# Latent tiles in the tables' loop and six normalisation tiles in the recurrence's last chunks

## The chip, the core and the metric

The kernel runs on one core of a Trainium2 chip. The metric is the device time of one execution in microseconds; of several runs the median counts. Engines are named as in the profile: PE is TensorE, PEld its weight loads, DVE is VectorE, ACT is ScalarE, POOL is GpSimd, SP is SyncE, which only starts DMAs here.

## What is computed

Two layers of a first block, then one layer of a second block (which the change doesn't touch), over 1024 tokens of width 1024; the first block works on T = 1040 tokens, 16 of them learned. A layer of the first block projects each token to 1920 + 448 features, feeds 448 of them to latent attention (four heads) and the rest to a recurrence that runs over the tokens in both directions (eight heads of 64 x 64 state), joins the two, and goes through a mixture of experts. The parts that matter here:

```python
proj = h @ w_in[li]
c_q, c_kv, k_pe, rw = _split(proj, [Q_LORA, KV_LORA, QK_ROPE, RWKV_COLS])   # 256, 128, 64, 1920
y_att = _mla(c_q, c_kv, k_pe, ...)          # rms norms of c_q and c_kv, rope of k_pe, softmax attention
u = p + mu_prev * (prev - p) + mu_next * (nxt - p)       # p = rw, shifted by a token both ways
r, k, v, wd_f, wd_b, ad_f, ad_b, gd = _split(u, [...])   # 512 each for r, k, v; 64 each; 128
v = v + (v_first - v) * sigmoid(v0 + (v @ v1) @ v2)      # in the second layer only
g = sigmoid(gd) @ g2
kk = k * k_k; kk = kk * rsqrt(sum(kk * kk, heads) + 1e-12)
for each direction:
    decay = exp(-exp(-softplus(-(w0 + tanh(wd) @ w2)) - 0.5)); a = sigmoid(a0 + ad @ a2)
    kd = k * (1 + (a - 1) * k_a)
    S = S * w_t - (S kk_t) (kk_t a_t)' + v_t k_t';  y_t = S r_t          # over the tokens
    bonus = sum(r * kd * r_k) * v
y = y_f + y_b; yn = (y - mean) * rsqrt(var + eps) * gn_g + gn_b          # by head
out = (yn + bonus_f + bonus_b) * g
```

## The kernel before

Features lie on partitions, tokens along the free axis. `proj` works in *feature tiles* of 128 columns of `w_in`. `ftile` splits a weight tile into a high and a low part (`pw_hi` on ACT, `pw_lo` on DVE) and makes 72 matmuls of 128 x 348 (three token thirds, eight steps of the inner dimension, three products of high and low parts), in one of the two PSUM buffers of tag `mm`. `shifted` copies the sum to SBUF on ACT (`pt`) and makes the shift by a token of three DVE steps: times `c0`, plus `mup` times the left neighbour, plus `mun` times the right one (L388 to L393). `plain` is `ftile` with a copy alone.

The order in `proj`: tiles 12 and 13 (`wd`, `ad`); then `dirs` with the k tiles 4 to 7, the norms of kk (`unit_keys`: `kk_ps`, a reciprocal, and `kkb_ps` with 12 products that scale all four kk), and the *tables' loop* over f = 0 to 3. A pass of it has the r tile f and, for both directions d, the low-rank products `low_ps` (first of `wd`, giving `lg`, then of `ad`, giving `ta`), a scan over the tokens (`cum`), an exponential (`P`), and the tables AR and BK, made by DVE and POOL, which ACT's queue stores to DRAM. The last DVE steps of a pass add and multiply kd (L612, L613), and PE's `bo` takes the bonus sum from them. After the loop come the v tiles 8 to 11 and `values`: in layer 1 the residual chain of v (a DMA of `vf`, two small products, a sigmoid and three DVE steps for each of the four tiles), then transposes `v_ps` of v forwards and reversed (`vr`, by POOL), copied by ACT and stored by ACT's queue. `latent` stands last: the tile of the rotary key (`kr`), tile 14 (the gate), the compressed keys' tile (`ck`) and two of compressed queries (`cq`), and between them, at the end of a tile's third third, the gate's rows `g_ps`, the norm of ck (`ck_ps`, a reciprocal) and the rotary product (`kp_ps`). This whole part is ordered by a scheduler that looks at priorities in program order and at free buffers.

`recur` is ordered by hand for PE, ACT, DVE and SP (`manual_schedule`); POOL is not in that list. It runs over N = 17 chunks of 64 tokens, one chunk of each direction at a time. Within a chunk c stand the state's product (`Rp`), the solve (`Wp`), own and next products (`dS`, and on DVE the state S, L968), and the output `Yp`, copied as `ys` by ACT and stored as `d_y` by POOL's queue. Beside them `r_inv` inverts the triangular blocks of four later chunks at once, in 31 double steps on DVE (L876, L877) and three transposes (Z, TF, TT). `turn` hands out these steps by an estimated time:

```python
left = turn(inv, left, 2.2)      # after C["solve"]
left = turn(inv, left, 0.8)      # after C["next"]
left = turn(inv, left, 99.0 if c % GRP == GRP - 1 else 5.2)   # after C["out"]; GRP = 4
```

`r_prep` builds blocks six and more chunks ahead, so the last chunks have none. `r_load` clears half of `uv` on POOL and loads the rest on SP's queue. After the loop `r_post` is called for nine token tiles (tile 0 has 16 tokens, the others 128): it loads both directions' y (POOL's queue), v and g (SP's), adds, takes mean and variance by head (DVE reduces, POOL subtracts, ACT squares and takes a root), scales, adds the bonus and multiplies by g, on DVE and POOL in turn, and stores `yr`. The scheduler places these steps among those of `mla`, the attention that follows, whose heads each run over nine query tiles (`ms` scores on PE, `mx` on DVE, Exp on ACT, `ptp` transposes).

## Time and profile before

| what | us |
| --- | --- |
| median of three runs | 4390.46 (4386.04 to 4396.25) |
| the profiled execution | 4402.54 |
| its span in the trace | 4400.7 |
| PE busy in it | 3830.7 (87%) |
| DVE busy | 2767.7 (63%) |
| ACT busy | 1869.7 (42%) |
| POOL busy | 988.2 (22%) |

The page gives each engine's busy time, a picture of the span in 40 slices, the DMA queues, the chain of work that ended last and the costliest groups of instructions. For a change that touches four stages the busy shares of the whole span say little; what counts is which engine is full in each stage, and which wait ends last. In layer 0 the k tiles and the loop lie between about 80 and 282 us, the projection's tail up to 402, the recurrence up to 679, the attention's heads from 725 on; in layer 1 the loop ends at 1819, the tail at 1969. A row of the timeline merges neighbours of one kind (x6 is six of them); the bracket behind it is the idle time of the engine before it and what ended that. An fp32 product stands in the trace as two matmuls.

### The profile page before, as it was taken

The numbers are of one execution on the slowest core, as the hardware profiler recorded it, in microseconds if no ns is written. First come the engines' busy times: TensorE is split into PE (matmuls) and PEld (weight loads), VectorE is DVE, ScalarE is ACT, GpSimd is POOL, SyncE is SP. The second block draws the span as 40 slices with busy tenths as digits, with TensorE's granted clock in tenths as the row PEclk, the third lists the DMA queues.
The fourth block names the chain that finished last, engine by engine and source line by source line (L and its number), as shares of the span: only waits on it lengthen the run. The fifth ranks groups of instructions, "written<-read, shape, count | busy, mean of one in ns | idle before, by whom it ended". The sixth has DMA issues, their size and how long they took to land. (4 is left out here: it accounts for less than half of the span.)

```text
span 4400.7 us, 68329 instructions
## 1 busy us (share of the span) xinstructions
PE 3830.7 (87%) x27155; PEld 3157.1 (72%) x27155; DVE 2767.7 (63%) x4684; ACT 1869.7 (42%) x3033; POOL 988.2 (22%) x719
## 2 busy tenths in 40 slices
PE   7888897899699688897887896997898889999998
PEld 7677676786576476776776775765786677888786
DVE  7763777757698757627668577997644753333354
ACT  4323445542387543233555532876424522111232
POOL 2331124201242243311233012331422410000000
PEclk9788798999799887886988997999998899999999
DMA  4446663113499833447641043998521121111232
GB/s 154 101 129 183 160 161 108 37 54 128 160 345 346 300 102 101 115 143 172 165 125 58 1 172 131 340 335 309 181 73 29 53 97 58 48 48 43 90 126 81
DMA packets 384153, 611.94 MB, mean 139 GB/s; under 512 B 50467, under 2 KB 217602, under 8 KB 381762
## 3 DMA queue, kind: packets, MB, share of 16 engines
q1 hardware_dynamic: 278402, 485.38, 35.3%
q10 hardware_dynamic: 85200, 70.97, 5.4%
q0 software_dynamic: 20224, 51.15, 3.7%
q8 instruction: 216, 3.54, 0.3%
q14 instruction: 111, 0.91, 0.1%
HBM read 491.65 MB, written 123.45 MB: 140 GB/s over the span
## 5 line engine op out<-in xcount | busy, mean ns | idle before, releaser
L252 DVE TENSOR_TENSOR w13l<-xw,w13h 128x1024 fp32r<-128x1024 f32 x248 | 296.4, 1220 | 57.5 <-ACT w13h L251 53.9
L251 ACT ACTIVATE w13h<-xw 128x1024 fp32r<-128x1024 f32 x256 | 267.4, 1058 | 130.3 <-PE x_hp L258 76.6
L256 PE MATMUL pp_ps<-T_hi,pw_hi 128*128 128x348 f32 x912 | 309.7, 340 | 8.7 <-ACT T_hi L1752 2.9
L257 PE MATMUL pp_ps<-T_lo,pw_hi 128*128 128x348 f32 x912 | 305.4, 335 | 1.4 <-DVE T_lo L1757 1.3
L258 PE MATMUL pp_ps<-T_hi,pw_lo 128*128 128x348 f32 x912 | 304.3, 334 | 0.0
L2414 PE MATMUL f_mm<-F_hi,f_wh 128*128 128x512 f32 x704 | 222.8, 398 | 1.7 <-ACT F_hi L251 1.7
L2414 PE MATMUL f_mm<-F_lo,f_wh 128*128 128x512 f32 x704 | 222.6, 397 | 0.0
L2414 PE MATMUL f_mm<-F_hi,f_wl 128*128 128x512 f32 x704 | 222.3, 397 | 0.0
L256 PE MATMUL x_hp<-w13h,x_h 128*96 128x512 f32 x512 | 208.5, 407 | 0.1
L257 PE MATMUL x_hp<-w13l,x_h 128*96 128x512 f32 x512 | 204.7, 400 | 0.0
L258 PE MATMUL x_hp<-w13h,x_l 128*96 128x512 f32 x512 | 204.0, 398 | 0.0
L256 PEld LDWEIGHTS pp_ps<-T_hi,pw_hi 128*128 128x128 f32 x912 | 179.8, 197 | 21.8 <-issue 7.8
L257 PEld LDWEIGHTS pp_ps<-T_lo,pw_hi 128*128 128x128 f32 x912 | 179.8, 197 | 5.1 <-DVE T_lo L1757 2.6
L287 POOL TENSOR_TENSOR g_x<-g_x,g2g 128x1024 f32<-128x1024 f32 x6 | 14.3, 2385 | 750.4 <-ACT g_x L284 750.4
L258 PEld LDWEIGHTS pp_ps<-T_hi,pw_lo 128*128 128x128 f32 x912 | 179.5, 197 | 3.0 <-issue 3.0
L252 DVE TENSOR_TENSOR f_wl<-F_raw,f_wh 128x1024 fp32r<-128x1024 f32 x44 | 53.7, 1221 | 203.2 <-ACT f_wh L251 203.2
L251 ACT ACTIVATE f_wh<-F_raw 128x1024 fp32r<-128x1024 f32 x44 | 46.4, 1060 | 307.0 <-PE f_mm L2414 301.4
L1616 POOL DMA_INDIRECT d_y<-x_o,r_idx x64 | 102.8, 1606 | 312.1 <-DVE x_al L252 288.8
L825 PE MATMUL aa<-ar_p,bk_p 64*128 64x128 f32 x1088 | 134.0, 376 | 40.2 <-DVE A L827 33.6
L2414 PEld LDWEIGHTS f_mm<-F_hi,f_wh 128*128 128x128 f32 x704 | 133.1, 189 | 34.4 <-ACT F_hi L251 2.0
L2414 PEld LDWEIGHTS f_mm<-F_lo,f_wh 128*128 128x128 f32 x704 | 132.7, 189 | 32.8 <-DVE F_lo L252 0.6
L2414 PEld LDWEIGHTS f_mm<-F_hi,f_wl 128*128 128x128 f32 x704 | 132.9, 189 | 32.4
(630 smaller groups left out, 11221.3 us busy)
## 6 DMA issues: line engine op xcount, KB each, us to landing
xw<-in_moe_w SPq DMA_DIRECT2D x256, 512.0 KB
xw<-in_moe_w SPq DMA_DIRECT2D x64, 1024.0 KB
wd_raw<-in_w_down SPq DMA_DIRECT2D x44, 512.0 KB
pw_raw<-in_w_in SPq DMA_DIRECT2D x36, 512.0 KB
d_AR<-AR ACTq DMA_DIRECT2D x32, 544.0 KB
d_BK<-BK ACTq DMA_DIRECT2D x32, 544.0 KB
ar_p<-d_AR SPq DMA_DIRECT2D x68, 256.0 KB
bk_p<-d_BK SPq DMA_DIRECT2D x68, 256.0 KB
```

The costliest lines, as they stand in the source:

```text
L251: nc.scalar.activation(hi, src, AF.Copy)
L252: (lo_eng or nc.vector).tensor_tensor(lo, src, hi.bitcast(F32), ALU.subtract)
L256: mm(out, wh, xh, start=first, stop=False)
L257: mm(out, wh, xl, start=False, stop=False)
L258: mm(out, wl, xh, start=False, stop=last)
L287: e1.tensor_tensor(out[:n], out[:n], gb[:n], ALU.mult)
L825: nc.tensor.matmul(aa[d][:, h - z], bk[q, h], ar[q, h], start=True, stop=True)
L1616: nc.gpsimd.indirect_dma_start(out=y2[:, :], out_offset=bass.IndirectOffsetOnAxis(ap=si, axis=0), in_=y, in_offset=None, bounds_check=2 * ...
L2414: nc.tensor.matmul(p[:, j], a[:, k], b[:, k, 512 * j:512 * j + 512], start=st, stop=sp)
```

## The change

- `shifted`: the product with `c0` moves from DVE to a second ACT copy that reads PSUM, with a scale.
- Four latent tiles (two of `cq`, `ck`, `kr`) move from the end of the projection into the loop: `compressed` is a generator, and each pass of the loop takes one tile from it after its first direction. `ck` and `kr` go to DRAM (`raw`) and are read back by `latent`. Each cq tile sums its squares by itself (`sqs`).
- The loop's beginning: the low-rank products run ahead, `lg` one direction ahead (two buffers), `ta` as soon as its buffer is free. The norms of kk stand ahead of the first r tile, and a pass scales its own kk alone.
- `latent` stands ahead of the v tiles, with loads and POOL's rope; the norm of ck and the rotary product run within v tile 1. Tile 14 follows the v tiles, the gate's rows stand between the forward transposes. The transposes are copied by DVE with four buffers and stored by SP's queue.
- `r_post` is a generator of four stages. Six tiles (4, 5, 3, 6, 2, 7) begin in chunks 10 to 15; every chunk takes a stage of each tile under way after `C["out"]` and another after the inverse's last turn. The add of both directions moves from POOL to DVE, the store of `yr` from ACT's queue to POOL's. Tiles 1, 8 and 0 follow the loop.

```diff
-                nc.vector.tensor_scalar(u, pt[:, 1:T + 1], p["c0"][:, j:j + 1], None, ALU.mult)
+                nc.scalar.activation(u.rearrange("p (q n) -> p q n", q=3), ps, AF.Copy, scale=p["c0"][:, j:j + 1])
+                u = u[:, :T]
...
+                self.dirs(li, p, S, psp, up, kp, shifted, wd, ad, lw, self.compressed(p, S, psp, up, cp, ftile))
             with self.tpool(name="p_v", bufs=1) as vp:
-                vt = [shifted(8 + f, vp.tile([128, T], F32, name=f"vt{f}", tag=f"val{f}")) for f in range(4)]
-                self.values(li, vt, p, S, psp, up, vp)
-                self.latent(li, p, S, psp, up, vp, shifted, ftile)
-
-    def latent(self, li, p, S, psp, up, vp, shifted, ftile):
+                norm, rotated, gate = self.latent(li, p, S, psp, up, vp, shifted)
+                vt = [shifted(8 + f, vp.tile([128, TP], F32, name=f"vt{f}"), {0: norm, 1: rotated} if f == 1 else {}) for f in range(4)]
+                gated = gate()
+                self.values(li, vt, p, S, psp, up, vp, gated)
...
+    def compressed(self, p, S, psp, up, cp, ftile):
...
+        for f in range(2):
+            a = plain([(128 * f, 128, 0)])
+            x = up.tile([128, TP], F32, name="u")[:, :T]
+            nc.scalar.activation(x, a, AF.Square)
+            sqs = psp.tile([128, 9, 2], F32, name="sqs", tag="tp")
+            for i, (c, n) in enumerate(TT):
+                nc.tensor.matmul(sqs[:n, i], x[:, c:c + n], self.ones32[:, 0:2], start=True, stop=True)
+            nc.scalar.activation(cqs[:NM, f, 0:1], sqs[:NM, 0, 0:1], AF.Copy)
+            nc.scalar.activation(cqs[:, f, 1:9], sqs[:, 1:9, 0], AF.Copy)
+            nc.vector.tensor_scalar(a, a, p["qn"][:, f:f + 1], None, ALU.mult)
+            nc.scalar.dma_start(S["cq"][f], a)
+            yield
+        for i, cols in enumerate(([(256, 128, 0)], [(384, 64, 0), (416, 32, 64), (384, 32, 96)])):
+            nc.scalar.dma_start(S["raw"][i], plain(cols))
+            yield
...
+        def decay(f, d):
+
+            lg = low(wd, lw["w2"], f, d, "lg", p[f"w0{d}h"], 2)
+            nc.gpsimd.tensor_scalar(lg, lg, -0.5 * CDEC, -0.5 * CDEC, ALU.mult, ALU.add)
+            return lg
+
+        def rate(f, d):
+            return low(ad, lw["a2"], f, d, "ta", p[f"a0{d}h"], 1)
...
+        ahead, ta1 = decay(0, 0), rate(0, 0)
+        norms()
         for f in range(4):
-            r = shifted(f, up.tile([128, T], F32, name="u"), {} if f else {0: norms, 2: scaled})
-            k, kk = kt[f], kkt[f][0]
+            k, kk = kt[f], scaled(f)
+            r = shifted(f, up.tile([128, TP], F32, name="u"))
             kds = []
             for d in range(2):
+                lg, ta = ahead, ta1
+                if f + d < 4:
+                    ahead = decay(f + d, 1 - d)
...
+                    ta1 = rate(f + d, 1 - d)
...
+                if d == 0:
+                    next(between)
...
-        def scaled():
-            for f in range(4):
-                for c, n in NC3:
-                    rb = psp.tile([128, 512], F32, name="kkb_ps", tag="tp")
-                    nc.tensor.matmul(rb[:, :n], self.pairpick[:, 128 * f:128 * f + 128], rn[:, c:c + n], start=True, stop=True)
-                    nc.vector.tensor_tensor(kt[f][0][:, c:c + n], kt[f][0][:, c:c + n], rb[:, :n], ALU.mult)
+        def scaled(f):
+            kk = kp.tile([128, T], F32, name="kk", bufs=2)
+            for c, n in NC3:
+                rb = psp.tile([128, 512], F32, name="kkb_ps", tag="tp")
+                nc.tensor.matmul(rb[:, :n], self.pairpick[:, 128 * f:128 * f + 128], rn[:, c:c + n], start=True, stop=True)
+                nc.vector.scalar_tensor_tensor(kk[:, c:c + n], kt[f][:, c:c + n], p["kk"][:, f:f + 1], rb[:, :n], ALU.mult, ALU.mult)
+            return kk
...
+                vs = vp.tile([128, RW], F32, name="v_sb", bufs=4)
+                nc.vector.tensor_copy(vs[:n], vp_ps[:n])
+                nc.sync.dma_start(S["v"][rev][c:c + n, :], vs[:n])
+                if not rev:
+                    next(gated)
...
+                order, rows = [4, 5, 3, 6, 2, 7, 1, 8, 0], []
+                rest = [self.r_post(R, i) for i in order]
+
+                def norms(c, new=False):
+                    if new and 10 <= c < 16:
+                        rows.append(rest.pop(0))
+                    for r in list(rows):
+                        if next(r, 0) == 0:
+                            rows.remove(r)
...
                     C["out"]()
+                    norms(c, True)
                     next(late, None)
                     if P:
                         P["diag"]()
                     left = turn(inv, left, 99.0 if c % GRP == GRP - 1 else 5.2)
+                    norms(c)
...
-        nc.gpsimd.tensor_tensor(y0[:n], y0[:n], y1[:n], ALU.add)
         yv = y0[:n].rearrange("p (h v) -> p h v", h=8)
         y1v = y1[:n].rearrange("p (h v) -> p h v", h=8)
         vv = v[:n].rearrange("p (h v) -> p h v", h=8)
         mu = tp.tile([128, 8], F32, name="q_mu")
+        vr = tp.tile([128, 8], F32, name="q_vr")
+        nc.gpsimd.tensor_tensor(vv, vv, S["bonus"][:n, i, :, None].to_broadcast([n, 8, 64]), ALU.mult)
+        nc.gpsimd.tensor_tensor(v[:n], v[:n], bb[:n], ALU.add)
+        yield
+        nc.vector.tensor_tensor(y0[:n], y0[:n], y1[:n], ALU.add)
         nc.vector.tensor_reduce(mu[:n], yv, AX.X, ALU.add)
         nc.vector.tensor_scalar(mu[:n], mu[:n], 1.0 / 64, None, ALU.mult)
         nc.gpsimd.tensor_tensor(yv, yv, mu[:n, :, None].to_broadcast([n, 8, 64]), ALU.subtract)
+        yield
         nc.scalar.activation(y1[:n], y0[:n], AF.Square)
-        vr = tp.tile([128, 8], F32, name="q_vr")
         nc.vector.tensor_reduce(vr[:n], y1v, AX.X, ALU.add)
+        yield
         nc.scalar.activation(vr[:n], vr[:n], AF.Sqrt, scale=1.0 / 64, bias=self.eps["gn"][:n])
         nc.vector.reciprocal(vr[:n], vr[:n])
-        nc.gpsimd.tensor_tensor(vv, vv, S["bonus"][:n, i, :, None].to_broadcast([n, 8, 64]), ALU.mult)
-        nc.gpsimd.tensor_tensor(v[:n], v[:n], bb[:n], ALU.add)
         nc.vector.tensor_tensor(yv, yv, vr[:n, :, None].to_broadcast([n, 8, 64]), ALU.mult)
         nc.vector.tensor_tensor(y0[:n], y0[:n], gb[:n], ALU.mult)
         nc.vector.tensor_tensor(y0[:n], y0[:n], v[:n], ALU.add)
         nc.gpsimd.tensor_tensor(y0[:n], y0[:n], g[:n], ALU.mult)
-        nc.scalar.dma_start(S["yr"][c0:c0 + n, :], y0[:n])
+        nc.gpsimd.dma_start(S["yr"][c0:c0 + n, :], y0[:n])
```

How the change stands in the program, at the places that the prediction speaks of. TensorE, layer 0, between the r tiles of pass 1 and pass 2 before (`pp_ps` are matmuls of feature tiles, `low_ps` low-rank products; the second s_wd row belongs to the other direction):

```order
L258 MATMUL pp_ps<-T_hi,pw_lo 128x348
L563 MATMUL low_ps<-s_wd,r_w_652 128x348 x3
L563 MATMUL low_ps<-s_ad,r_a_654 128x348 x3
L563 MATMUL low_ps<-s_wd,r_w_652 128x348 x3
L616 MATMUL bo<-rkp,kd 16x2
L616 MATMUL bo<-rkp,kd 128x2 x8
L563 MATMUL low_ps<-s_ad,r_a_654 128x348 x3
L256 MATMUL pp_ps<-T_hi,pw_hi 128x348
```

The same engine now, from the end of pass 0 to the latent tile of pass 1. Ahead of these rows stand the latent tile of pass 0, and r tile 1 with `sqs` and `bo` between its matmuls:

```order
L258 MATMUL pp_ps<-T_hi,pw_lo 128x348
L670 MATMUL kkb_ps<-kk_rn,pairpick 128x346
L559 MATMUL low_ps<-s_wd,r_w_652 128x348 x2
L670 MATMUL kkb_ps<-kk_rn,pairpick 128x346
L559 MATMUL low_ps<-s_wd,r_w_652 128x348
L559 MATMUL low_ps<-s_ad,r_a_654 128x348 x3
L256 MATMUL pp_ps<-T_hi,pw_hi 128x348
```

Before, low-rank products and `bo` follow one another with nothing of a tile between; now a pass has 144 `pp_ps` instead of 72, `bo` stands within the next r tile, and a pass's own `kkb_ps` are among the low-rank products.

TensorE, layer 0, near the projection's end before (the last tile with the gate's last rows, then the first sums of squares, after which `aa`, the recurrence's first product, follows):

```order
L256 MATMUL pp_ps<-T_hi,pw_hi 128x348
L486 MATMUL g_ps<-g_2313,gd 128x512
L257 MATMUL pp_ps<-T_lo,pw_hi 128x348
L258 MATMUL pp_ps<-T_hi,pw_lo 128x348
L493 MATMUL ck_ps<-ck_sq,ones_2311 128x348
L493 MATMUL ck_ps<-ck_sq,ones_2311 128x346 x2
L486 MATMUL g_ps<-g_2313,gd 128x512
L513 MATMUL sqs<-ones_2311,cq_sq_2707 16x2
L513 MATMUL sqs<-ones_2311,cq_sq_2802 16x2
```

And now, behind the last matmul of tile 14 (`vt` are the v tiles, `gd` is the gate):

```order
L258 MATMUL pp_ps<-T_hi,pw_lo 128x348
L717 MATMUL v_ps<-ident,vt_2274 16x128
L717 MATMUL v_ps<-ident,vt_2379 16x128
L717 MATMUL v_ps<-ident,vt_2465 16x128
L518 MATMUL g_ps<-g_2170,gd 16x512
L717 MATMUL v_ps<-ident,vt_2188 128x128
L717 MATMUL v_ps<-ident,vt_2274 128x128
L717 MATMUL v_ps<-ident,vt_2379 128x128
L717 MATMUL v_ps<-ident,vt_2465 128x128
L518 MATMUL g_ps<-g_2170,gd 128x512
```

The gate's rows and the transposes stood among the latent tiles' matmuls; now they follow the last tile, a gate row after each row of four transposes, then the reversed transposes and `aa`.

VectorE, end of chunk 11 and begin of chunk 12 before (TF and TT are the inverse's last transposes, Z and `tm` begin the next inverse, S is the state):

```order
L880 STREAM_TRANSPOSE TF<-Tn 128x32x32
L883 STREAM_TRANSPOSE TT<-Tn 128x32x32
L968 TENSOR_TENSOR S_2888<-dS,pend_2883 128x512
L870 STREAM_TRANSPOSE Z<-dc 128x1024
L876 TENSOR_TENSOR tm<-Z,Tn 128x31
L877 TENSOR_TENSOR Tn<-Tn,tm 128x31
L876 TENSOR_TENSOR tm<-Z,Tn 128x60
L877 TENSOR_TENSOR Tn<-Tn,tm 128x30x2
L968 TENSOR_TENSOR S_2889<-dS,pend_2883 128x512
```

And now, from the same transposes on (`q_y`, `q_vr` and `q_mu` belong to the normalisation tiles):

```order
L928 STREAM_TRANSPOSE TF<-Tn 128x32x32
L931 STREAM_TRANSPOSE TT<-Tn 128x32x32
L1016 TENSOR_TENSOR S_2898<-dS,pend_2893 128x512
L1058 TENSOR_REDUCE q_vr<-q_y_5720 128x8
L1061 RECIPROCAL q_vr<-q_vr 128x8
L1062 TENSOR_TENSOR q_y_5719<-q_y_5719,q_vr 128x512
L1063 TENSOR_TENSOR q_y_5719<-q_y_5719,gn_g 128x512
L1064 TENSOR_TENSOR q_y_5719<-q_y_5719,q_v 128x512
L1052 TENSOR_TENSOR q_y_5893<-q_y_5893,q_y_5894 128x512
L1053 TENSOR_REDUCE q_mu<-q_y_5893 128x8
L1054 TENSOR_SCALAR q_mu<-q_mu 128x8
L918 STREAM_TRANSPOSE Z<-dc 128x1024
```

The S of chunk 11 stays behind TT; a tile's last stage and the next tile's second one stand between it and the next inverse. A stage that begins a chunk's second half (L1058) stands among the inverse's steps, as do the second and fourth stages of the chunks whose inverse has steps left.

## Rows read from the trace of the kernel before

**Rows 1.** Busy time of each engine in three stretches (columns in the first line; x counts instructions):

```profile
core 0: us, PE busy (x) PEld busy (x) DVE busy (x) ACT busy (x) POOL busy (x), PEclk, DMA share, GB/s
209.00:246.00 37.00, 30.18 (x125) 24.21 (x124) 26.53 (x26) 12.33 (x15) 18.53 (x12) 0.68 0.64 158
350.00:402.00 52.00, 50.66 (x292) 43.95 (x290) 9.13 (x6) 21.47 (x34) 9.05 (x7) 0.97 0.40 139
700.00:760.00 60.00, 41.12 (x215) 36.32 (x214) 53.52 (x83) 29.53 (x61) 32.52 (x28) 0.80 0.29 82
```

**Rows 2.** Timeline of TensorE at the loop's start (start us, us, engine line op, operands, shapes):

```profile
119.70 0.32 PE L257 MATMUL pp_ps<-T_lo,pw_hi 128*128 128x348 f32 x1
...
121.78 0.32 PE L258 MATMUL pp_ps<-T_hi,pw_lo 128*128 128x348 f32 x1
...
122.02 1.94 PE L629 MATMUL kk_ps<-kk_sq,pair 128*32 128x348 f32 x6
...
142.94 7.05 PE L638 MATMUL kkb_ps<-kk_rn,pairpick 128*128 128x346 f32 x16
...
151.21 0.42 PE L256 MATMUL pp_ps<-T_hi,pw_hi 128*128 128x348 f32 x1 [1.22 <-ACT ta L565]
```

**Rows 3.** Timeline of VectorE, the last step of passes 0 and 3:

```profile
173.39 1.23 DVE L613 TENSOR_TENSOR kd<-kd,u 128x1040 f32<-128x1040 f32 x1
...
279.57 1.23 DVE L613 TENSOR_TENSOR kd<-kd,u 128x1040 f32<-128x1040 f32 x1
```

**Rows 4.** Timeline: ends of the loop and of the projection, layer 0, then layer 1:

```profile
280.85 2.44 PE L616 MATMUL bo<-rkp,kd 128*16 128x2 f32 x12 [7.63 <-DVE kd L613]
...
402.25 0.76 PE L825 MATMUL aa<-ar_p,bk_p 64*128 64x128 f32 x2 [1.60 <-DMA bk_p<-d_BK]
...
1856.43 1.02 ACT L390 ACTIVATE pt<-pp_ps 128x1044 f32<-128x1044 f32 x1
...
1896.16 1.24 DVE L671 SCALAR_TENSOR_TENSOR vt<-vf,vt 128x1040 f32<-128x1040 f32 x1
...
1969.07 0.77 PE L825 MATMUL aa<-ar_p,bk_p 64*128 64x128 f32 x2 [1.08 <-DMA bk_p<-d_BK]
```

**Rows 5.** Groups of TensorE's instructions, 350 to 381 (count | busy us, mean ns | idle):

```profile
L684 PE MATMUL v_ps<-ident,vr 128*128 128x128 f32 (+1 forms) x32 | 4.1, 272 | 0.0
```

**Rows 6.** Groups of VectorE's instructions in passes 1 to 3:

```profile
L593 DVE SCALAR_TENSOR_TENSOR BK<-ta,cum 128x1024 f32<-128x1024 f32 x6 | 13.9, 2311 | 0.1
...
L588 DVE TENSOR_TENSOR kd<-kd,k 128x1040 f32<-128x1040 f32 x6 | 7.4, 1227 | 0.0
```

**Rows 7.** Timeline: a VectorE step beside GpSimd's, first head:

```profile
715.36 6.93 DVE L1099 TENSOR_TENSOR qs<-qpe,qs 64x1040 fp32r<-64x1040 f32 x1
...
720.16 1.03 POOL L1009 TENSOR_TENSOR q_v<-q_v,s_bonus 128x512 f32<-128x512 f32 x1
```

**Rows 8.** Groups of VectorE's instructions in the last chunks, 618.7 to 671:

```profile
L876 DVE TENSOR_TENSOR tm<-Z,Tn 128x207 f32<-128x207 f32 (+15 forms) x40 | 13.2, 330 | 2.2 <-POOL Tn L868 1.0
```

**Rows 9.** Timeline of VectorE, an S step of the last chunks:

```profile
641.84 0.69 DVE L968 TENSOR_TENSOR S<-dS,pend 128x512 f32<-128x512 f32 x1 [8.28 <-PE dS L966]
```

**Rows 10.** Waits of VectorE, 607 to 682 (us in total, times, longest):

```profile
DVE cql L252 <- ACT cqh L251: 9.0, 1, 9.0
```

**Rows 11.** Groups of VectorE's and GpSimd's instructions in the first heads, 690 to 815:

```profile
L1012 DVE TENSOR_TENSOR q_y<-q_y,gn_g 128x512 f32<-128x512 f32 (+1 forms) x8 | 5.3, 668 | 0.0
...
L1009 POOL TENSOR_TENSOR q_v<-q_v,s_bonus 128x512 f32<-128x512 f32 x7 | 8.9, 1269 | 3.5 <-DMA q_v<-d_v 3.5
```

**Rows 12.** Timeline of ScalarE, first Exp of heads 0, 2, 3, last of head 3:

```profile
725.18 1.28 ACT L1155 ACT_TABLE_LOAD   x1 [13.98 <-DVE mx L1152]
...
858.09 0.93 ACT L1155 ACTIVATE Pm<-ms,mx,s_rq 16x696 f32<-16x696 f32 x1 [1.56 <-DVE mx L1152]
...
925.70 0.91 ACT L1155 ACTIVATE Pm<-ms,mx,s_rq 16x696 f32<-16x696 f32 x1
...
974.33 0.93 ACT L1155 ACTIVATE Pm<-ms,mx,s_rq 128x696 f32<-128x696 f32 x1 [0.41 <-DVE mx L1152]
```

More of the change, by code (lines that the diff above doesn't have):

```diff
@@ L510, in latent, with rotated @@
-        sqs = psp.tile([128, 9, 2], F32, name="sqs", tag="tp")
-        for i, (c, n) in enumerate(TT):
-            for f in range(2):
-                nc.tensor.matmul(sqs[:n, i], sq[f][:, c:c + n], ones[:, 0:2], start=f == 0, stop=f == 1)
-        nc.scalar.activation(rq[:NM, 0:1], sqs[:NM, 0, 0:1], AF.Sqrt, scale=1.0 / 256, bias=self.eps["rms"][:NM])
-        nc.scalar.activation(rq[:, 1:9], sqs[:, 1:9, 0], AF.Sqrt, scale=1.0 / 256, bias=self.eps["rms"])
+        def rotated():
+            ps = psp.tile([128, 3, 512], F32, name="kp_ps", tag="mm")
+            c3(lambda q, c, n: nc.tensor.matmul(ps[:, q, :n], dup, kr[:, c:c + n], start=True, stop=True))
+            k2 = vp.tile([128, T], F32, name="kp", tag="val0")
+            c3(lambda q, c, n: nc.scalar.activation(k2[:, c:c + n], ps[:, q, :n], AF.Copy))
+            nc.scalar.dma_start(S["ckv"][1], k2)
@@ new lines, in gate, with rows @@
+        def gate():
+            u = shifted(14, up.tile([128, TP], F32, name="u"))
+            gd = vp.tile([128, T], F32, name="gd", tag="sq")
+            nc.scalar.activation(gd, u, AF.Tanh, scale=0.5)
+            nc.vector.tensor_scalar(gd, gd, 0.5, 0.5, ALU.mult, ALU.add)
+            def rows():
+                for c, n in TT:
+                    gp = psp.tile([128, 512], F32, name="g_ps", tag="tp")
+                    nc.tensor.matmul(gp[:n], gd[:, c:c + n], g2, start=True, stop=True)
+                    gs = vp.tile([128, RW], F32, name="g_sb", bufs=2)
+                    nc.scalar.activation(gs[:n], gp[:n], AF.Copy)
+                    nc.scalar.dma_start(S["g"][c:c + n, :], gs[:n])
+                    yield
+            return rows()
@@ L518, in latent, with dirs @@
         nc.vector.tensor_scalar(nrq, rq, -1.0, None, ALU.mult)
-    def dirs(self, li, p, S, psp, up, kp, shifted, wd, ad, lw):
+        return norm, rotated, gate
+    def dirs(self, li, p, S, psp, up, kp, shifted, wd, ad, lw, between):
         nc = self.nc
@@ L529, in dirs, with low @@
             nc.vector.tensor_scalar(rkp[:, f], self.pair, p["rk"][:, f:f + 1], None, ALU.mult)
[L530 removed]
+        kt, sqs = [], []
         for f in range(4):
[L532 to L538 removed]
+            k = shifted(4 + f, kp.tile([128, TP], F32, name=f"k{f}"))
+            sq = kp.tile([128, T], F32, name=f"kk_sq{f}", tag=("kk", "cum", "kd", "P")[f], bufs=2 if f == 0 else None)
+            nc.scalar.activation(sq, k, AF.Square, scale=p["kk"][:, f:f + 1])
+            kt.append(k), sqs.append(sq)
+        norms, scaled = self.unit_keys(kt, sqs, p, psp, kp)
+        def low(x, wt, f, d, nm, bias, bufs):
+            ps = psp.tile([128, 3, 512], F32, name="low_ps", tag="mm")
+            for q in range(3):
+                nc.tensor.matmul(ps[:, q, :348], wt[64 * d:64 * d + 64, 128 * f:128 * f + 128],
+                                 x[64 * d:64 * d + 64, 348 * q:348 * q + 348], start=True, stop=True)
+            out = kp.tile([128, TP], F32, name=nm, bufs=bufs)
+            nc.scalar.activation(out.rearrange("p (q n) -> p q n", q=3), ps[:, :, :348], AF.Tanh, scale=0.5, bias=bias[:, f:f + 1])
+            return out
+        def decay(f, d):
[4 more added lines that the diff above has]
+            return low(ad, lw["a2"], f, d, "ta", p[f"a0{d}h"], 1)
         AR = [kp.tile([128, 17, 2, 64], F32, name=f"AR{d}") for d in range(2)]
@@ L558, in both @@
                     fn(dst[:, 16 * d, slot, 0:NM], [x[:, o:o + NM] for x in srcs])
-                def low(x, wt, out, bias):
-                    ps = psp.tile([128, 3, 512], F32, name="low_ps", tag="mm")
-                    for q in range(3):
-                        nc.tensor.matmul(ps[:, q, :348], wt[64 * d:64 * d + 64, 128 * f:128 * f + 128],
-                                         x[64 * d:64 * d + 64, 348 * q:348 * q + 348], start=True, stop=True)
-                    nc.scalar.activation(out.rearrange("p (q n) -> p q n", q=3), ps[:, :, :348], AF.Tanh, scale=0.5, bias=bias)
-                lg = kp.tile([128, TP], F32, name="lg")
-                low(wd, lw["w2"], lg, p[f"w0{d}h"][:, f:f + 1])
-                nc.gpsimd.tensor_scalar(lg, lg, -0.5 * CDEC, -0.5 * CDEC, ALU.mult, ALU.add)
                 cum = kp.tile([128, T], F32, name="cum")
@@ L628, in norms @@
                 for q, (c, n) in enumerate(NC3):
[L629 removed]
+                    nc.tensor.matmul(ss[32 * f:32 * f + 32, q, :n], self.pair32, sqs[f][:, c:c + n], start=True, stop=True)
             for q, (c, n) in enumerate(NC3):
@@ L673, in values @@
             if rev:
-                vr = [vp.tile([128, T], F32, name=f"vr{f}") for f in range(4)]
+                vr = [vp.tile([128, T], F32, name=f"vr{f}", tag=f"val{f}") for f in range(4)]
                 for f in range(4):
@@ L800, in recur @@
                         C = Cn
-            for i in range(9):
-                self.r_post(R, i)
+            for r in rows + rest:
+                for _ in r:
+                    pass
     def r_fetch(self, pool, names, S, ch):
```

80 lines of the change are left out of this document (25 added, 55 removed).

## The prediction

> **What bounds the kernel now.** I read busy shares and granted clock of single stretches first, then single rows at the places that the change touches. TensorE is the busiest engine of the whole span, but that share hides four stages with different limits, and the change works on all four, once in each of the two layers.
>
> In the tables' loop (four passes f in `dirs`) nothing is full. In one pass of 37 us TensorE is busy 30.18 us at a mean granted clock of 0.68, VectorE 26.53, GpSimd 18.53 [rows 1]. A pass takes 35.4 us: the last VectorE step of pass 0 starts at 173.39 and that of pass 3 at 279.57 [rows 3], and 106.18 / 3 = 35.4. The pass is a ring over the engines: `bo` waited 7.63 us for VectorE [rows 4]. The projection's tail is the opposite: from 350 to 402 TensorE is busy 50.66 of 52 us at 0.97 [rows 1], so a matmul taken from there is worth its whole time. In the recurrence's last chunks VectorE sets the pace: inverse steps (L876, L877) and transposes follow one another, and its long idle pieces are 8.28 us before one S and 9.0 us behind the loop [rows 9, 10]. In the first attention heads, where the normalisation tiles run now, VectorE is busy 53.52 of 60 us [rows 1].
>
> **Part 1: four latent tiles out of the tail.** Fourteen matmuls of a feature tile start between 119.70 and 121.78: 13 steps in 2.08 us, 0.16 us each [rows 2]; 72 make 11.5 us. Four tiles are 46 us of full tail per layer. They go into the loop, one in each pass.
>
> What a pass costs then: TensorE gets 11.5 us for the tile, three `kkb_ps` (a product of this kind is two matmuls in the trace; 16 took 7.05 us [rows 2], so six take 2.6) and in two of the four passes nine `sqs` (18 matmuls at the 0.2 us of `bo`, 12 in 2.44 [rows 4]; 3.7): 16 us on average, against 6.8 us that it idles in a pass. By this alone the pass is 35.4 + 9.2 = 44.6. The clock gives something back: 30.18 us of work at 0.68 is 20.5 us at full speed, so that the pass would hold 20.5 and some 15 us at best. VectorE gets three scalings of kk, each a third of a product of 1.23 us, and one low half of weights (as a whole product), and loses the scale by c0, which ScalarE now does from PSUM: +1.2 to +2.5 us by the 1.23 of L588 [rows 6] on its 26.53, so it is not the bound. Ends: 37 us, if the tile fills waits alone at a full clock and VectorE's addition is all that shows; 46, if the sum from idle time holds, the clock stays and the ring adds a little. I take 41, between them: the tile runs where TensorE waits, and some 3.6 us come back by the clock.
>
> The first pass gets shorter. Now `kk_ps` is issued at 122.02 inside r tile 0, and r tile 1 starts only at 151.21, behind the `kkb_ps`, which wait for VectorE's scalings and whose last 16 matmuls start at 142.94 [rows 2]. After the change the norms stand ahead of most of r tile 0 (about 4.5 us earlier, k's last square being there by 117.5), and one pass's scalings instead of four stand in front (about 7 us less). So pass 0 ends 11.5 us earlier, three passes add 5.6 each, and `bo` of pass 3 starts at 286 instead of 280.85 [rows 4].
>
> Layer 0 from there: the program still has 299 matmuls of tiles (48 us), `bo` and the products of norm and rope (each like `kk_ps`, 1.94 [rows 2]), so tile 14 ends near 339. Then work stands bare that was covered: the gate's chain (two copies at 1.02 as the one in [rows 4], two shifts at 1.23, tanh as a copy, a scale; with hand-overs near 7 us), nine rows of `g_ps` with the forward transposes, and the reversed transposes. Eight matmuls, a row's four transposes, take 1.0 us of TensorE (32 in 4.1 [rows 5]), and I put the gate's product at another 1.0, so eight rows are 16 us and the reversed ones 8. The recurrence's first `aa` comes at 339 + 31 = 370 to 372 instead of 402.25 [rows 4]: **-31 us** (-11 at a pass of 46, -47 at 37).
>
> Layer 1 has the residual chain behind the v tiles: from the copy of v tile 3 at 1856.43 to the last vt at 1896.16, 40 us [rows 4]. The latent tiles cover it now; then tile 14 covers 11.5 us of it. From v tile 3's end to `aa` I count 11.5 + 37 (the chain behind tile 14) + 14 (transposes left) + 7.5 = 70 us, where it took 1969.07 - 1856.43 = 112.6 [rows 4]. That is -42.6; the loop's end moves by +5, and the v tiles start with about 7 us less of them done beside the loop, since the latent tile takes that room: **-30 us**. Both layers: -61.
>
> **Part 2: six normalisation tiles into chunks 10 to 15.** A tile costs VectorE an add (moved here from GpSimd), two reduces and three products at 0.67 [rows 11], a scale and a reciprocal: 4.5 us. It costs GpSimd four operations at 1.27 [rows 11], 5.1 us. By the order of stages, chunk 10 holds 1.6 us of it for VectorE and 3.8 for GpSimd, chunks 11 and 15 a reduce ahead of their inverse's end (0.67 and 2.5 each), chunks 12 to 14 a whole tile each (13.5 and 15.3). What stands behind the last transpose of chunks 11 and 15 lies in the idle 8.28 and 9.0 us [rows 9, 10] and costs nothing; without that cover it would be 3.8 us each. Exposed: 16.4 us of VectorE less 2 us of short idle time, 14.4, and 24.1 us of GpSimd that runs beside it.
>
> Whether GpSimd's time counts is the open cost. Rows of the loop show VectorE operations with two inputs in SBUF standing still while GpSimd computes: BK (L593) takes 2.31 us on average where kd (L588), as long, takes 1.23 [rows 6]; `qs` took 6.93 us, until GpSimd's operation at 720.16 was done [rows 7]. The inverse steps have two SBUF inputs too, but no row of before shows them beside GpSimd's arithmetic: so from nothing (+14 us) to all of it (+39). L876, with L877 as long, fills some 27 of these 52 us [rows 8], and the products of the tiles add to it, so I count 0.6 of 24.1: +29 us per layer. The Trainium skill, SBUF — State Buffer, section Who interferes with whom, has a VectorE instruction with two SBUF inputs and a GpSimd instruction that reads SBUF block each other in full; rows 6 and 7 agree with it, and it speaks for the +39 of rival (b).
>
> GpSimd's queue: its memsets of `uv` and the `d_y` stores stand behind the new steps, but a chunk holds 2.1 us of them and 5.1 us of new work, and lasts 8 us and more; so they come later in the chunk without setting its pace. Square and root on ScalarE, about 1 us a tile, I cost at nothing: it waits for S most of a chunk; if not, +6 a layer.
>
> Given back: two heads, from the first Exp at 725.18 + 1.28 to that of the third at 858.09, take 131.6 us with the nine tiles beside them; the last head needs 974.33 - 925.70 = 48.6 us for eight of its nine blocks, so 54.7 [rows 12]. So up to 131.6 - 109.4 = 22 us, or nothing, if other work fills the room. With three tiles left I take **13**. Part 2: +29 - 13 = +16 per layer, +32.
>
> **The sum.** -61 + 32 = -29 on the profiled execution's 4402.54 us: 4373.5. That execution lies 12.1 us above the median of the runs, 4390.46; set against the median, the forecast is **4361 us**.
>
> **The rivals.**
> (a) GpSimd doesn't hold the inverse steps: +14 instead of +29 per layer, -59 in all, 4331. For it: the steps take a third of a microsecond each [rows 8], and GpSimd may find its time between them.
> (b) All of its time is added: +39 per layer, so -9, 4381. For it: `qs` in [rows 7].
> (c) Slower: the latent tile lies on the loop's ring at the lower clock. At a grant of 0.68 [rows 1] a tile costs 17 us, not 11.5; a pass of 46 is 5 above the forecast, times four passes and two layers +40, so +11, 4402. The gain is used up at 44.6 us a pass. Against it: the tile is placed just where TensorE waits.
> (d) The norms leave the heads, and these don't get shorter, because the softmax's steps on VectorE and ScalarE follow one another anyway: +26, so -3, 4387.
>
> **How the numbers follow.** 0.2% is 8.8 us, about what a measurement of this kernel can tell from no change. Forecast 0.42 (faster 0.34, same 0.06, slower 0.02); (a) 0.18, all faster; (b) 0.12 (0.06, 0.05, 0.01); (c) 0.17 (0.01, 0.02, 0.14); (d) 0.11 (0.04, 0.05, 0.02). Faster 0.63, same 0.18, slower 0.19. The range ends above just past (c), 4404, and below between (a) and (a) with a pass of 37 (32 less): 4315.
>
> **What the profile after would show.** Part 1 is right if the last VectorE step of a pass comes every 41 us or less and the first `aa` near 371, in layer 1 some 30 us earlier; wrong if the passes take 44.6 or more. Part 2 is right if the time from chunk 10's S to the last `ys` grows by 29 us and the first two heads shrink to near 119. Inverse steps stretched beside GpSimd's rows would show (b), unstretched ones (a). All of it would be wrong if the gate's or layer 1's chain stood in the open for much longer than 7 and 37 us.

## The result and the profile after

The change makes the kernel slower: 4419.25 us (median of four runs, 4416.21 to 4421.55) against 4390.04; the ratio is 1.0062, 95% interval 1.0047 to 1.0076. The forecast was 4361, with 4315 to 4404 as its range; the time lies above it. The profiled execution took 4420.4 us, near its median, where that of the kernel before lies 12 us above its own; so a stage-by-stage comparison of the two traces treats the new kernel some 10 us too kindly. Those us are in a stretch that the change doesn't touch, from the last attention head to layer 1's projection (739 us in the trace of before, 723 to 734 in those of the other kernels with the same output).

The page's first rows for the kernel after:

```profile
span 4418.6 us, 68340 instructions
## 1 busy us (share of the span) xinstructions
PE 3802.8 (86%) x27155; PEld 3127.4 (71%) x27155; DVE 2773.2 (63%) x4710; ACT 1850.4 (42%) x3008; POOL 963.4 (22%) x719
```

They explain nothing: every engine has about as much work as before, and the span is longer. The stages do (us, layer 0 / layer 1):

| stretch | before | after | forecast |
| --- | --- | --- | --- |
| one pass of the loop (mean of passes 1 to 3) | 35.4 / 34.9 | 44.9 / 46.2 | 41 |
| last VectorE step of pass 3 to first `aa` | 122.7 / 151.5 | 100.3 / 129.2 | 86 / 116 |
| reciprocal of the kk norms to first `aa` | 276.8 / 304.0 | 278.9 / 310.4 | -31 / -30 |
| first `aa` to S of chunk 8 | 196.1 / 197.4 | 188.8 / 190.5 | 0 |
| S of chunk 8 to S of chunk 15 | 72.2 / 72.0 | 96.6 / 98.0 | +29 |
| S of chunk 15 to first Exp of head 0 | 56.0 / 51.1 | 74.5 / 73.6 | 0 |
| first Exp of head 0 to that of head 3 | 199.2 / 198.2 | 169.5 / 172.2 | -13 |

(The first part's forecast stands in the third row; in the second row it is worked out from the prediction's terms. The chunks are numbered from 0; 8 and 9, which have no tile, are in the fifth row on both sides. The heads' forecast is that of the first two.) The projection was to give 61 us and takes 8.5; the recurrence, the start of attention and the heads were to cost 32 us and cost 21 by these rows (+5.9 in layer 0, +15.6 in layer 1).

**The loop.** VectorE's last step of passes 0 to 3, the rows that answer to [rows 3]:

```profile
168.22 1.23 DVE L645 TENSOR_TENSOR kd<-kd,u 128x1040 f32<-128x1040 f32 x1
214.35 1.17 DVE L645 TENSOR_TENSOR kd<-kd,u 128x1040 f32<-128x1040 f32 x1
261.94 1.23 DVE L645 TENSOR_TENSOR kd<-kd,u 128x1040 f32<-128x1040 f32 x1
302.94 1.23 DVE L645 TENSOR_TENSOR kd<-kd,u 128x1040 f32<-128x1040 f32 x1
```

Pass 0 ends 5.2 us earlier than before, and passes 1 to 3 take 46.1, 47.6 and 41.0 us. Busy time in these three (columns as in [rows 1]):

```profile
168.00:214.00 46.00, 39.15 (x195) 32.77 (x194) 30.56 (x34) 20.64 (x27) 18.99 (x12) 0.85 0.56 132
214.00:262.00 48.00, 43.28 (x220) 36.57 (x219) 29.52 (x36) 16.42 (x18) 18.32 (x13) 0.89 0.51 127
262.00:303.00 41.00, 34.73 (x203) 31.27 (x201) 31.04 (x31) 15.09 (x17) 18.76 (x11) 0.95 0.51 117
```

The clock rose from 0.68 to 0.85, 0.89 and 0.95, yet the passes grew. TensorE isn't slow; it is idle for 5 to 7 us of each pass. VectorE and GpSimd are idle for longer, and ScalarE, the one that they wait for below, is busy for less than half. The chain between them shows in the timelines of ScalarE (with its DMA issues, ACTq) and of VectorE at one place of pass 1:

```profile
189.43 1.13 ACT L562 ACTIVATE ta<-low_ps,phalf 128x1044 f32<-128x1044 f32 x1 [7.36 <-DVE AR L627]
189.51 1.24 ACTq L640 DMA_DIRECT2D d_BK<-BK  x2
190.87 5.58 ACTq L640 DMA_DIRECT2D d_AR<-AR  x2
196.50 1.07 ACT L606 ACTIVATE P<-cum 128x1040 f32<-128x1040 f32 x1 [5.94 <-issue]
```

```profile
189.44 2.33 DVE L603 TENSOR_TENSOR_SCAN cum<-zm,lg 128x1040 f32<-128x1040 f32 x1
191.72 0.06 DVE L605 MEMSET P<- 128x1 f32 x1
197.60 3.47 DVE L625 TENSOR_TENSOR AR<-kk,P 128x1024 f32<-128x1024 f32 x2 [5.83 <-ACT P L606]
```

The scan that P needs ends at 191.77. P starts at 196.50, when ScalarE's queue has issued two stores of AR: 5.58 us for two, where the two of BK before them took 1.24. "issue" is the bracket's word for an engine that waits for nothing but its own queue. VectorE then waits 5.83 us for P. The stores of the next AR hold the queue once more, now because that table isn't made yet; the copy `pt` of the latent tile stands behind the first of them, and TensorE's low-rank products wait for `pt`. Waits of ScalarE and of TensorE from 120 to 303 us (total, times, longest):

```profile
ACT P L606 <- issue: 17.4, 3, 5.9
...
PE low_ps L559 <- ACT pt L446: 13.5, 3, 6.8
```

Before, P waited for an issue once (3.1 us), and TensorE's longest wait in the loop was the one of [rows 4] for kd. But work stood behind these stores already: at the end of passes 2 and 3 the weights' copy `pw_hi` did, for 10.8 us each time. ScalarE's queue in the trace of before:

```profile
275.18 1.29 ACTq L610 DMA_DIRECT2D d_AR<-AR  x2
279.72 2.48 ACTq L610 DMA_DIRECT2D d_BK<-BK  x2
282.25 1.06 ACT L251 ACTIVATE pw_hi<-pw_raw 128x1024 fp32r<-128x1024 f32 x1 [10.80 <-issue]
```

Of the 10.80 us the issues take 3.8; for the rest the queue waits until the tables that it is to store are made. So a wait for an "issue" can have two parts.

**The tail.** TensorE behind tile 14 in layer 0:

```profile
364.77 0.32 PE L258 MATMUL pp_ps<-T_hi,pw_lo 128*128 128x348 f32 x1
...
373.08 1.89 PE L518 MATMUL g_ps<-g,gd 128*16 128x512 f32 x2 [7.67 <-DVE gd L513]
...
385.57 1.12 PE L518 MATMUL g_ps<-g,gd 128*128 128x512 f32 x2 [3.27 <-ACT g_sb L520]
...
403.24 1.01 PE L873 MATMUL aa<-ar_p,bk_p 64*128 64x128 f32 x12 [0.85 <-DVE v_sb L719]
```

From tile 14 to `aa` it is 38.5 us (31 forecast): the gate's chain holds TensorE for the 7 us that were counted, but the gate's rows take 22 us (373 to 395) instead of 16, with six waits for ScalarE's copies `g_sb` (6.8 us). Three of these copies wait in turn for the store of an earlier row to free one of their two buffers, the longest here:

```profile
384.92 0.60 ACT L520 ACTIVATE g_sb<-g_ps 128x512 f32<-128x512 f32 x1 [4.24 <-DMA d_g<-g_sb]
```

The stretch ahead of it, from the last `bo` to the end of tile 14, is longer than forecast too: 60.9 us in place of 53.

**Chunks and handoff.** VectorE at the end of chunk 13, and GpSimd beside it:

```profile
654.21 2.42 DVE L924 TENSOR_TENSOR tm<-Z,Tn 128x247 f32<-128x247 f32 x1
656.66 0.42 DVE L925 TENSOR_TENSOR Tn<-Tn,tm 128x247 f32<-128x247 f32 x1
657.00 0.68 DVE L1016 TENSOR_TENSOR S<-dS,pend 128x512 f32<-128x512 f32 x1
```

```profile
654.31 1.04 POOL L1055 TENSOR_TENSOR q_y<-q_y,q_mu 128x512 f32<-128x512 f32 x1
655.31 1.04 POOL L1049 TENSOR_TENSOR q_v<-q_v,s_bonus 128x512 f32<-128x512 f32 x1
```

The inverse step, 0.4 us long as its neighbours are, takes 2.42: it ends just after GpSimd's two products, which take 2.0 together. As a group these steps average 501 ns (330 in [rows 8]):

```profile
L924 DVE TENSOR_TENSOR tm<-Z,Tn 128x207 f32<-128x207 f32 (+15 forms) x40 | 20.0, 501 | 1.1
```

Behind the last chunk ScalarE stands still (ScalarE, VectorE, then TensorE):

```profile
711.50 0.63 ACT L1057 ACTIVATE q_y<-q_y 128x512 f32<-128x512 f32 x1 [13.38 <-POOL q_y L1055]
712.16 0.60 ACT L1022 ACTIVATE ys<-Yp 128x512 f32<-128x512 f32 x1
```

```profile
708.73 0.69 DVE L1052 TENSOR_TENSOR q_y<-q_y,q_y 128x512 f32<-128x512 f32 x1 [13.43 <-DMA q_y<-d_y]
```

```profile
717.84 1.24 PE L1102 MATMUL ms<-cqh,wqh 128*128 128x348 f32 x3 [17.68 <-ACT wqh L251]
```

A square of tile 1 (L1057) stands ahead of the last `ys` and of the weights' high parts in ScalarE's queue. It waits for GpSimd's subtraction, this for VectorE's sum, this for the load of y, and the load is issued late on GpSimd's queue, behind a store of `yr`. Attention's first product waits 17.68 us for it. The heads then run faster: the first Exp of head 0 is at 763.11, of head 2 at 863.92, 100.8 us for two heads, where before it was 131.6.

### The profile page after: what moved, and what is told of

Its sections match the earlier page's. It is cut to its first block, busy times and chain, and to the rows that moved or that the text cites. A ratio compares the mean times of both kernels' runs of the same rounds, so it can differ in the third digit from the quotient of the medians.

```text
span 4418.6 us, 68340 instructions
## 1 busy us (share of the span) xinstructions
PE 3802.8 (86%) x27155; PEld 3127.4 (71%) x27155; DVE 2773.2 (63%) x4710; ACT 1850.4 (42%) x3008; POOL 963.4 (22%) x719
## 4 chain that ended last, share of the span: by engine, by line
PE 37%; DVE 6%; ACT 2%; DMA 2%; issue 2%; POOL 1%; SPq 0%; ACTq 0%; DVEq 0%; POOLq 0%
PE f_mm L2466 11%; PE a_ft L2038 3%; PE ms L1200 2%; PE g_mm L256 2%; PE g_mm L257 2%; PE g_mm L258 2%; DMA xw<-in_moe_w 2%; PE x_hp L256 1%; PE x_hp L257 1%; PE x_hp L258 1%; PE o_mm L256 1%; PE o_mm L257 1%; PE o_mm L258 1%; PE u_mm L258 1%; PE d_s L2241 1%
```

## The experiments

**One half each.** `e1_proj_only` has the new projection with the old recurrence and `r_post`; `e2_norms_only` has it the other way round.

> Only the projection's half of the change; the recurrence and the normalisation tiles stay as before. Theory A (the halves add up, as the stage times of the changed kernel suggest: projection +1 and +6 us, the recurrence's start -7 in each layer, some -14 between the layers): about 4382 us, 0.998 of before; passes of the loop stay at 41 to 48 us, first aa near 403 and 1969. Theory B (the slowdown of the loop is caused by the other half, for instance through buffers or the order): passes near 40 us and about 4335 us.

> Only the normalisation tiles' half; the projection stays as before. Theory A: chunks 8 to 15 about 24 us longer a layer, the step from the last S to the first Exp 18 to 22 us longer, the first two heads 27 to 31 us shorter: +13 to +22 a layer, 4425 us, 1.008 of before. Theory B (the tiles pay for themselves and the projection's half makes the loss): 4380 to 4392.

Measured: 4414.46, ratio 1.0052 (1.0035 to 1.0068), and 4417.25, ratio 1.0055 (1.0038 to 1.0071). Each half alone is slower. The projection's half was expected to be faster by both theories and costs 22 us; its passes take 46.0 in both layers. (Each run was measured with the kernel before beside it, at 4388.63 to 4392.57 us; the ratios are to that.) The halves add up to 47 us, and both together cost 29.

**The stores' queue.** `e5_tables_sp` is the changed kernel with the tables stored by SP's queue; `e8_before_sp` makes the same edit in the kernel before, and `e9_proj_sp` in `e1_proj_only`.

```diff
-                    nc.scalar.dma_start(S[nm][d][:, :, 2 * f + h], t[64 ...
+                    nc.sync.dma_start(S[nm][d][:, :, 2 * f + h], t[64 ...
```

> The changed kernel with the loop's stores of AR and BK issued by SP's queue instead of ScalarE's. Theory A (ScalarE stands behind these stores, 17.4 us in layer 0's loop ahead of the exponential alone, and that sets the pass): passes of 40 to 42 us instead of 46 to 48, 15 to 25 us less in both layers, about 4400. Theory B (the pass is set by VectorE, GpSimd and the low-rank products' buffers, the stores only fill waiting time; or SP's weight loads now stand behind the stores): passes stay at 44 or more, 4410 to 4430.

> The kernel before with the stores of AR and BK issued by SP's queue. Theory A (the stores cost much only in the new order, where the next exponential stands behind them on ScalarE; before, it waited for VectorE's scan): 4380 to 4396, passes 34 to 36 us. Theory C (the stores on ScalarE's queue hold the loop whatever the order, and the gain of the run with SP's queue has nothing to do with the change): passes near 30 us and about 4350.

> The projection's half alone, with the stores of AR and BK on SP's queue; normalisation tiles as before. Theory A (the projection's half loses by the stores alone, 42 us in two layers; the tiles' half costs some 20): 4414 - 42 = 4372 or a little less, passes 40 to 42. Theory B (the gain seen with both halves hangs on the tiles in the recurrence): 4385 or more.

Measured: 4377.06 (0.9971, 0.996 to 0.9981), 42 us below the changed kernel; 4388.04 (0.9994, 0.998 to 1.0007), no change; 4353.81 (0.9924, 0.9904 to 0.9945), 61 us below `e1_proj_only` (58 when each is set against the kernel before beside it) and below both kernels of this case. Passes take 37.6 in both layers of `e5_tables_sp`, and 37.6 / 37.9 in `e9_proj_sp`; `aa` comes at 384.67 in layer 0. The same place in `e9_proj_sp`, SP's queue and ScalarE:

```profile
188.26 1.28 SPq L640 DMA_DIRECT2D d_BK<-BK  x2
189.64 10.57 SPq L640 DMA_DIRECT2D d_AR<-AR  x4
```

```profile
188.29 1.14 ACT L562 ACTIVATE ta<-low_ps,phalf 128x1044 f32<-128x1044 f32 x1 [9.89 <-DVE AR L627]
190.72 1.07 ACT L606 ACTIVATE P<-cum 128x1040 f32<-128x1040 f32 x1 [1.29 <-DVE P L605]
```

The issue is no quicker there: the first two of these stores of AR take 2.42 and 3.08 us, where on ScalarE's queue they took 2.45 and 3.09. But P runs inside it. TensorE is then busy 44.90 of the 46 us of this window (39.15 in the changed kernel):

```profile
168.00:214.00 46.00, 44.90 (x229) 38.01 (x229) 36.35 (x40) 21.64 (x27) 18.80 (x14) 0.89 0.67 163
```

Over passes 1 to 3 of layer 0 it is busy 109.5 of 112.9 us, so a pass is now little longer than TensorE's own work in it. Both runs of the new order gained more than theory A had. So the stores on ScalarE's queue cost the new order some 8 us in each of passes 1 to 3, and the old order nothing that shows in the total, though its passes, too, get some 2 us shorter (33.2 / 33.1).

**Latent tiles behind the loop.** `e7_latent_behind` is `e9_proj_sp` with the four tiles after the loop.

```diff
-                if d == 0:
-                    next(between)
...
+        for _ in between:
+            pass
```

> As the run before (projection's half, stores on SP), but the four latent tiles stand behind the loop instead of in it. Theory A (with the stores out of ScalarE's way the tiles fill TensorE's waits in the loop): passes 33 to 36 us, but 46 us more behind the loop: 15 to 30 us slower than with the tiles inside. Theory B (a tile in a pass costs what it costs behind, 11.5 us each): within 8 us of the run before.

Measured: 4412.77 (1.0057, 1.0038 to 1.0077), 59 us above `e9_proj_sp`. The passes stay at 38.3 / 36.8, not the 33 to 36 expected, and the stretch from pass 3 to `aa` grows from 106.8 to 141.2 (layer 0) and from 137.2 to 174.3 (layer 1), 34.4 and 37.1. Pass 0 does get shorter without its tile: from the reciprocal of the kk norms to the end of pass 3 the loop takes 4 us less in layer 0 and 8 in layer 1. So four tiles in the loop cost 4 to 8 us once ScalarE is free, and are worth 34 to 37 in the tail. This is the first part's claim, shown by itself. (Without the tiles TensorE doesn't set the passes: GpSimd's BK waits 34.3 us, in five waits, for stores of BK to free its buffer.)

**Low-rank products back in their old places,** everything else as in `e1_proj_only`, with the stores on ScalarE.

```diff
-                lg, ta = ahead, ta1
-                if f + d < 4:
-                    ahead = decay(f + d, 1 - d)
+                lg = decay(f, d)
...
+                ta = rate(f, d)
```

> The projection's half alone with the stores on ScalarE's queue as in the change, but the low-rank products back in their old places in each direction (not ahead). Theory A1 (the products drawn ahead make ScalarE ready early, so that its queue stands behind the stores; without them the exponential waits for the scan as before): passes 40 to 42 us and about 4370. Theory A2 (the stores hold ScalarE wherever the products stand, because there is more behind them in a pass with a latent tile, copies above all): passes 45 us or more and 4405 to 4425.

Measured: 4466.5 (1.0176, 1.0152 to 1.02), passes of 52, slower than either theory had it. ScalarE's waits, from 120 to 330 us:

```profile
ACT pw_hi L251 <- issue: 40.3, 3, 13.9
```

Here a pass's weights stand behind the stores instead of P. Of a wait of 13.8 us, the one that ends at 201.59, 7.1 us are the queue's wait for the tables and 6.7 the issue of four stores. Running ahead was not the mistake; it limits the damage.

**GpSimd taken out of the chunks.** `e10_no_gpsimd` is `e2_norms_only` without the four GpSimd operations of a tile; the output differs, and with it the experts' loads, so only the chunks can be compared.

```diff
-        nc.gpsimd.tensor_tensor(vv, vv, S["bonus"][...], ALU.mult)
-        nc.gpsimd.tensor_tensor(v[:n], v[:n], bb[:n], ALU.add)
-        nc.gpsimd.tensor_tensor(yv, yv, mu[...], ALU.subtract)
-        nc.gpsimd.tensor_tensor(y0[:n], y0[:n], g[:n], ALU.mult)
```

> The kernel with the tiles' half alone, and GpSimd's four operations of a normalisation tile left out (subtraction of the mean, bonus, its sum and the product with g), so that the output is another. Theory A (GpSimd holds VectorE's inverse steps; the steps' mean of 501 against 330 ns says some 8 us a layer): S of chunk 8 to S of chunk 15 takes 88 to 91 us instead of 98. Theory B (all of GpSimd's time counted, 24 us): 74 to 80. Theory C (no hold): 96 or more.

Measured (one execution): from S of chunk 8 to that of chunk 15 88.15 us in layer 0 (98.4 in `e2_norms_only`, 72.2 before) and 91.5 in layer 1 (97.3 and 72.0). Layer 0 fits theory A, layer 1 lies just above it. Some of the inverse's steps in the two, `e10_no_gpsimd` first (614 to 678 us), then `e2_norms_only` (619 to 696):

```profile
L889 DVE TENSOR_TENSOR tm<-Z,Tn 128x247 f32<-128x247 f32 (+15 forms) x44 | 14.8, 336 | 1.3
```

```profile
L889 DVE TENSOR_TENSOR tm<-Z,Tn 128x220 f32<-128x220 f32 (+15 forms) x41 | 18.3, 447 | 1.2
```

Without GpSimd's arithmetic they are about as short as in [rows 8]: all 120 steps of this stretch, L889 and the one behind it, take 41.5 us in either layer, as before, and 51.0 / 49.7 in `e2_norms_only`. So GpSimd's part is 10.3 us in layer 0 and 5.8 in layer 1 (the waits of a tile on GpSimd went with it, too), and 16 / 19.5 us are left for the tiles' own steps.

**Start of the tiles.** `e4_seven` lets the seventh tile begin in chunk 16; `e12_three_tiles` (stores on SP) has three tiles in the chunks instead of six.

```diff
-                    if new and 10 <= c < 16:
+                    if new and 10 <= c < 17:        # e4_seven
+                    if new and 13 <= c < 16:        # e12_three_tiles
```

> The changed kernel with one tile more in the recurrence: tile 1 begins in chunk 16, so that its square on ScalarE stands behind the last ys by hand instead of ahead of it by the scheduler. Theory A (the last ys and the attention's first splits wait on ScalarE behind that square, which waits for a load): the last ys comes 10 to 12 us earlier after the last S, 16 to 24 us less in all, about 4398. Theory B (the handoff is long because VectorE still works off the tiles, whatever the order on ScalarE): within 6 us of 4419.

> Both halves, stores on SP's queue, but three normalisation tiles in chunks 13 to 15 instead of six in chunks 10 to 15. Theory A (each tile in a saturated chunk costs about 4 us there and 2 to 3 at the handoff, and gives back less than 5 in the heads): between the run with none (4354) and the one with six (4377), 4360 to 4370. Theory B (only the first tiles are dear, since they delay the next inverse): 4345 to 4354.

Measured: `e4_seven` 4417.44 (1.0059, 1.0042 to 1.0077). The last `ys` comes 12 us sooner after S of chunk 15 (11.6 us, not 23.5), but the first Exp only 6 and 4 us sooner, and the total doesn't move. So the square ahead of `ys` is only one of the things that hold the start of attention: its first product, too, starts 12 us sooner, but from there to the first Exp it now takes 52 and 53 us, where it was 45 and 44 in the changed kernel and 44 and 39 before. `e12_three_tiles` 4371.91 (0.9955, 0.9938 to 0.9973): 5 us below the six tiles of `e5_tables_sp`, which the two intervals don't tell apart, and 18 above the none of `e9_proj_sp`. It lies just above theory A's range.

**The gate before the last v tile,** in layer 0 of `e9_proj_sp`, with four buffers for its rows.

```diff
+                    if f == 3 and li == 0:
+                        gated = gate()
```

> The projection's half with the stores on SP's queue, and in layer 0 the gate's tile ahead of the last v tile, with four buffers instead of two for the gate's rows. Theory A (the tail behind the last tile waits 7.7 us for the gate's chain and 7 us for the rows' copies and stores): 8 to 15 us less than the 4354 without this, first aa of layer 0 at 370 to 377. Theory B (the last v tile's own chain and the loads of the recurrence's tables set aa): within 4 us of 4354.

Measured: 4352.48 (0.991, 0.9886 to 0.9935), `aa` at 384.32 instead of 384.67. The time is theory B's. The 7.67 us that TensorE waited for the gate were not what set `aa`; what does was not tried.

## Why the prediction was wrong

**The pass of 41 us is the step that failed.** It was bounded by TensorE's idle time (44.6 to 46) and by VectorE's addition (37), and measured 44.9 and 46.2. ScalarE had no term: the product with `c0` was taken from VectorE and "which ScalarE now does from PSUM" was all that was said of it there, and the stores that the loop issues from ScalarE's queue were not looked at, though `pw_hi` stood 10.8 us behind them in the trace of before. An issue is no busy time; ScalarE, at 12.33 of 37 us [rows 1], looked free. In the old order what stood behind the stores cost the pass some 2 us (`e8_before_sp`). With two tiles and low-rank products ahead in each pass P, `pt` or `pw_hi` stands there, and each holds the engine that waits for it. The chip shows it from both sides: on SP's queue the passes take 37.6, near the forecast's lower end, pass 0 ends 8 to 10 us earlier than before (5.2 in the changed kernel, 11.5 forecast), and the time falls by 42 and 61 us; the same edit in the old order gives nothing clear. From the reciprocal of the kk norms to `aa`, moving the stores gives 26 and 24 us in the projection's half, 50 of its 61.

**The tail** is the second step, and the stores don't explain it. The loop's end came 18 us later than forecast in layer 0 and 24 in layer 1; the rest of the miss, 14 and 13 us, lies between it and `aa` (second row of the table). With the stores on SP's queue this stretch is longer still, 107.0 and 136.3. In layer 0 it is 8 us ahead of tile 14's end: the terms named there, 299 matmuls, `bo` (18 products, 3.72 us) and two products of 1.94, make 55 us rather than 53, and TensorE waits besides. Behind tile 14 it was 31 us by its terms and took 38.5 (in layer 1 58, and 67): in layer 0 the gate's chain as counted, the gate's rows 6 us longer for ScalarE's copies and their stores. Layer 1 has the same loop to pay for, 3 x 11.3 us in passes 1 to 3, and loses its 22 us gain of the tail in it.

**Rival (c)** gave a pass of 46 and 4402. Its length came and its reason didn't: the low clock was to make the tile dear, but the clock rose to 0.85 and more, and without the stores a tile costs 1 to 2 us in the loop (`e7_latent_behind`). Had only the length been read, (c) would pass for confirmed.

**The chunks** were sized at +29 and took 24 to 26. VectorE's part, 14.4, measured 16 and 19.5; GpSimd's, 0.6 of its time or 14.5, measured 10.3 and 5.8. So the truth stands between (a) and the forecast, and (b) is out. The Trainium skill, SBUF — State Buffer, section Who interferes with whom, has a VectorE instruction with two SBUF inputs and a GpSimd instruction that reads SBUF exclude each other; the row at 654.21 agrees with it. The stage shows that only part of GpSimd's time falls on such an instruction: beside 24 us of its arithmetic the inverse's steps get 8 to 10 us longer. By the prediction's own sign, from chunk 10's S to the last `ys`, part 2 looks dearer, +38 and +39 us in place of 29; 15 of these are the last `ys` behind tile 1's square, which belong to the handoff.

**The handoff** was costed at nothing, since what stood behind the last transposes lay "in the idle" of [rows 10], and square and root "at nothing". It costs 18.5 and 22.5 us (in the kernels that keep the old `r_post` this stretch lies between 51 and 58 us, so each is good to a few us). Idle time of VectorE covered VectorE's steps, but not the chain VectorE, GpSimd, ScalarE of a tile that begins there; ScalarE works in order and has the weights of attention behind it. `e4_seven` moves the head of that chain and not its end: which of its links sets the first Exp is open.

**The heads** gave back 26 to 30 us, 27 to 31 in the first two alone, instead of 13, more even than the bound of 22. That bound took 54.7 us for a head without tiles, from the last one; head 0 now takes 43.6 (763.11 to 806.71). Handoff and heads can't be parted cleanly, since what is late at the first Exp can be made up behind it: from S of chunk 15 to the first Exp of head 3 the two together give 11 us in layer 0 and 4 in layer 1. Rival (d) is out.

**Not foreseen:** `aa` to S of chunk 8 is 7 us shorter in both layers. The norm of ck, whose reciprocal of 6.65 us stood on VectorE at the recurrence's beginning, is done in v tile 1 now. That it is the reason is not shown: this stretch lies between 189 and 196 us in the nine kernels with the new projection and between 193 and 197 in the four with the old one, by the means a difference of 4 us.

**Open:** the halves cost 22 and 25 us alone and 29 together. With the stores on SP they do add up (-36 and +25 would be -11, and `e5_tables_sp` is 13 to 15 below the kernel before), so it is the new projection with ScalarE's stores that costs less in company. From the reciprocal to `aa` it costs 7 us a layer in `e1_proj_only` and 2 and 6 in the changed kernel; beside that the heads of `e1_proj_only` take 9 and 4 us longer than before, though no edit touched them (with the old `r_post` they take 198 to 209 us over all runs). Why, no run tells. Nor was the product with `c0` tried on VectorE again in the new order.

## What to carry to other kernels

Before work is moved into a loop that "waits anyway", list what each in-order queue will have ready, its DMA issues among it: a store that costs little while nothing urgent stands behind it sets the pace once something does, and no busy share shows it. Here the change of one word, which queue stores the tables, turns the first part from +22 to -36 us, and `e9_proj_sp` at 4353.81 is the version to keep, without the second part. And where a length comes out as a rival said, look whether its reason did.
